# Hybrid encoder step: index products ordered by operand, a new order of the first loads, and two planner constants

## The chip, the cores and the metric

One Trainium2 chip, one core of it. The metric is the device time of one execution of the kernel in microseconds (us). The kernel before was timed three times; the median is the time to compare with.

## What is computed

One layer of a streaming encoder in fp32: 512 prompt tokens and 32 sample tokens of width 1024, 256 memory tokens, and caches of keys and values of the past. One combined input projection feeds three groups of heads and an indexer; the heads' outputs are gated, projected out and added to x.

```python
def _mixer_inputs(x, g, w_in, pos):
    z = _rmsnorm(x, g) @ w_in
    qa, ka, va, ga, qb, kb, vb, gb, qm, gm, qi, ki, wi = _split_cols(z)
...
def _indexer_scores(qi, ki, wi):
    dots = jnp.einsum('bqhd,bsd->bqhs', qi, ki).astype(jnp.float32) * (D_IDX ** -0.5)
    w = wi.astype(jnp.float32) * (H_IDX ** -0.5)
    return jnp.einsum('bqh,bqhs->bqs', w, jax.nn.relu(dots))

def _gather_attend(q, k, v, scores, topk):
    top_val, top_idx = lax.top_k(scores, topk)
...
def _merge(x, oa, ob, om, ga, gb, gm, w_out):
    o = jnp.concatenate([oa * jax.nn.silu(ga), ob * jax.nn.silu(gb), om * jax.nn.silu(gm)], axis=-1)
    return x + o @ w_out
```

Group A is attention over a band of chunks with a position bias, B attends to the keys that the indexer picks, M attends to the memory tokens. Prompt and sample each have all three.

## The kernel before

**Products.** A product of fp32 precision is made of three matmuls. x is split into xTh (rounded, by ScalarE) and xTl (the rest, by VectorE), a weight tile `raw` into wh (ScalarE) and wl (VectorE for the first four pairs of tiles, GpSimd after that); h·wh, h·wl and l·wh are summed in one PSUM bank. The names stand in the rows: `bank<-wl,xTh` is the product of xTh with wl. x and weights have eight tiles of 128 rows along the width of 1024 (index k).

**Order of the work.** The program opens with the index projection (296 columns of `w_in`), which needs all of x: `x_load` sends the eight tiles of x_t (544 columns: 512 prompt, 32 sample) and the eight weight tiles on SP's queue, `x_split` and `w_split` split them, and `index_group` multiplies, for each k, three query tiles of 128 tokens. (The key part of the fourth tile is made apart by `key0` with the scaled weights `gw`.) After it come the input projections of the other groups (the first is ka), each with a small part for the sample tokens by `w_sample` (`bank<-raw,xF`, plain fp32 from the unsplit weights), then attention, and the output projections: the prompt's `bank<-wh,oAh`, `wh,oMh`, `wh,oBh` and the sample's `bank<-raw,oS` (`out_sample`). The sample's group B (`sample_b`) multiplies cached keys, `bank<-keysB,qbS`, that three loads of 512 KB bring in.

**Who sets the order.** The kernel is written out by a planner, `Line`. It keeps an estimated clock for each engine and runs many generators; one emits its next instructions when the planner's clocks say that its inputs are there. The order on each engine's queue is thus fixed when the program is built, by estimates: a DMA is put down with its bytes over 330e3 bytes per us (`Line.op`, line 249), and a PSUM bank counts as free 0.7 us after the estimated end of its last reader (`room` and `there`, lines 462 and 472). On the chip, semaphores keep the order right whatever the estimates were.

**Fillers.** `warm` (line 909) puts matmuls of a tile of ones on TensorE where the planner sees it wait during the index projection, until the time at which the next product is due, and `LATER` = 0.3 us beyond it.

All engine instructions go through one helper, so each row has the line L400; they are told apart by tiles.

Of the kernel before, what the change touches and what calls it, by code (L numbers as in the profile page):

```python
# [18 lines left out]
P = 128  # L19
# [6 lines left out]
NK = 8  # L26
NT = S // P
# [64 lines left out]
class Line:  # L92
# [139 lines left out]
    def op(self, eng, op, outs, ins, kw):  # L232
        deps = {}
        outs_, ins_ = ([x for x in xs if x.tensor.name in self.writes] for xs in (outs, ins))
        for x in outs_ + ins_:
            b = self.box(x)
            for w, o in self.writes[x.tensor.name]:
                if all(p[0] < q[1] and q[0] < p[1] for p, q in zip(w, b)):
                    if o.eng is None:
                        for u in o.users.values():  # L240
                            deps.setdefault(u, False)
                    else:
                        deps[o] = True
        for x in outs_:
            b = self.box(x)
            for (w, _), o in self.reads[x.tensor.name].items():
                if all(p[0] < q[1] and q[0] < p[1] for p, q in zip(w, b)):
                    deps.setdefault(o, False)
        d = (outs[0].size() * 4 / 330e3 if eng == "SP" else
             self.cost(eng, op, outs, ins, kw) * (1.0 if eng == "PE" else SLACK))  # L250
        share = eng == "POOL" or eng == "DVE" and self.shares(op, outs, ins)
        new = Op(eng, d, share, [(o, w) for o, w in deps.items()])
        for x in outs_:
            n, b = x.tensor.name, self.box(x)
            self.writes[n] = [e for e in self.writes[n]
                              if not all(q[0] <= p[0] and p[1] <= q[1] for p, q in zip(e[0], b))] + [(b, new)]
            self.reads[n] = {k: o for k, o in self.reads[n].items()
                             if not all(q[0] <= p[0] and p[1] <= q[1] for p, q in zip(k[0], b))}
        for x in ins_:
            self.reads[x.tensor.name][self.box(x), eng] = new  # L260
        for x in outs_ + ins_:
            self.users[x.tensor.name][eng] = new

        now = self.now()
        for q in self.queue.values():
            while q and q[0].start <= now:
                q.popleft().enter(self.base)
        self.queue[eng].append(new)
        if share and self.queue["POOL" if eng == "DVE" else "DVE"]:
            self.last = self.base.copy()  # L270
            self.events()
        else:
            self.begin(new, self.start(new))
# [155 lines left out]
def hybrid_step(ctx: ExitStack, tc: tile.TileContext, a: dict):  # L429
# [28 lines left out]
    def room(k=1):  # L458

        yield from line.wait(lambda: len(free_banks) >= k)  # L460
        while True:
            t = sorted(pp.free(f"b{b}") for b in free_banks)[k - 1] + 0.7
            if t <= line.now():
                return
            yield t
            yield from line.wait(lambda: len(free_banks) >= k)
# [2 lines left out]
    waiting = []  # L469

    def there(k):
        return k == 0 or len(free_banks) >= k and sorted(pp.free(f"b{b}") for b in free_banks)[k - 1] + 0.7 <= line.now()

    def divided(k, issue):

# [324 lines left out]
    def x_load():  # L800

        c = len(x_raw)
        yield from ()
        t = (rp.tile([P, 2, N], F32, tag="xr", name="xr", bufs=3) if c < 3 else
             cp.tile([P, 2, N], F32, tag="gate1", name="xr"))
        if c % 2 == 0:
            firsts.append(cp.tile([P, 2, 2, 296], F32, tag=("q0", "gate0")[c // 2], name="raw"))
        raw = firsts[c // 2][:, c % 2]
        for kk in range(2):
            rows = slice((2 * c + kk) * P, (2 * c + kk + 1) * P)  # L810
            if c == kk == 0:
                DMA.dma_start(gT[0], a["norm_mix_g"])
            DMA.dma_start(t[:, kk, :], a["x_t"][rows, :])
            DMA.dma_start(raw[:, kk, :], w_in[rows, QI:QI + 296])
        raws.append(raw)
        x_raw.append(t)

# [88 lines left out]
    ones = cp.tile([P, P], F32, tag="q2", name="ones")  # L906
    V.memset(ones, 1.0)

    def warm(until):
        fill, line.warm = line.warm, None  # L910
        until += LATER if until - line.clk["PE"] > WARM else 0
        while until - line.clk["PE"] > WARM:
            PE.matmul(idle[:, 0:P], ones, ones, start=True, stop=True)
        line.warm = fill
# [144 lines left out]
    def index_group():  # L1059
        acc = take(NT)  # L1060
        for c in range(NK // 2):
            w = w_next()
            for kk in range(2):
                k = 2 * c + kk
                line.until(lambda: x_k[0] > k and w_k[0] > k)
                wh, wl = (x[:, kk, :] for x in w)
                for t in range(1, NT):
                    h, l = (x[k // 4][:, k % 4, t * P:(t + 1) * P] for x in (xTh, xTl))
                    o = acc[t][:, 0:296]
                    yield wh, wl, h, l  # L1070
                    PE.matmul(o, h, wh, start=k == 0, stop=False)
                    PE.matmul(o, h, wl, start=False, stop=False)
                    PE.matmul(o, l, wh, start=False, stop=k == NK - 1)
                    if k == NK - 1:
                        line.spawn(i_done(t, acc[t]))
        line.spawn(key0(acc[0]))

    line.spawn(start())
# [1041 lines left out]
```

## Time and profile before

| | us |
|---|---|
| median of 3 runs (353.04, 354.0, 354.1) | 354.0 |
| the profiled execution | 353.58 |
| its span, first to last instruction | 351.8 |
| TensorE (PE) busy | 343.6 (98%) |
| VectorE (DVE) busy | 277.8 (79%) |
| ScalarE (ACT) busy | 220.8 (63%) |
| GpSimd (POOL) busy | 178.7 (51%) |
| mean granted TensorE clock | 0.998 of full speed |

The profile is of one execution; 1.8 us of its time lie outside the span. A row of the timeline gives the start of a group of like instructions, the time from its first start to its last end, the engine and the tiles; matmuls overlap in their pipeline, so the distance of two starts says more than the length of one. In a wait, the arrow names the instruction or DMA that ended it.

### The profile page before, as it was taken

To read this page: it belongs to the slowest core of one execution; us is meant where nothing else is said; L and a number is where in the kernel's file an instruction comes from. 1 tells how busy PE (TensorE), PEld (TensorE's weight loads), DVE (VectorE), ACT (ScalarE), POOL (GpSimd) and SP (SyncE) were. 2 spreads that over 40 slices of the span, in tenths; PEclk is the share of its full clock that TensorE was granted. 3 is DMA by queue.
4 is the path that set the end of the run, shared out by engine and by line. 5 is a ranking of instruction groups with operands and counts; after the bars stand their busy time and mean duration, and the time that the engine had idled before them with its cause. 6 is when DMAs were issued, how large, how long until landed. Compare 5 with 4: busy or idle time off the path is not lost.

```text
span 351.8 us, 7548 instructions
## 1 busy us (share of the span) xinstructions
PE 343.6 (98%) x2744; PEld 299.2 (85%) x2744; DVE 277.8 (79%) x706; ACT 220.8 (63%) x528; POOL 178.7 (51%) x195
## 2 busy tenths in 40 slices
PE   8999999999999999999999999999999999999992
PEld 7989978999999988887988998999986767676782
DVE  3765988878999979998999727999995689786543
ACT  5756777997767776786764328414793377663452
POOL 2569094475575557274654484552382064307542
PEclk9999999999999999999999999999999999999999
DMA  7999452375548223252131341234273185200024
GB/s 241 310 365 352 100 182 60 112 199 149 149 133 286 62 62 113 55 156 85 48 91 45 92 144 42 56 88 144 65 287 133 45 271 176 111 2 2 0 75 178
DMA packets 39604, 46.31 MB, mean 132 GB/s; under 512 B 5360, under 2 KB 32624, under 8 KB 39568
## 3 DMA queue, kind: packets, MB, share of 16 engines
q1 hardware_dynamic: 39568, 45.85, 41.8%
q8 instruction: 21, 0.34, 0.4%
q14 instruction: 15, 0.12, 0.1%
HBM read 39.67 MB, written 6.16 MB: 130 GB/s over the span
## 4 chain that ended last, share of the span: by engine, by line
PE 93%; DMA 3%; issue 1%; SPq 1%; DVE 1%; ACT 0%; POOLq 0%; POOL 0%; DVEq 0%; ACTq 0%
PE bank L400 93%; DMA keysB<-in_cache_b_k_dram 2%; DMA xr<-in_x_t_dram 1%; SPq L400 1%; DVE xr L400 0%; ACT sq L400 0%; POOLq L2108 0%; DVE wl L400 0%; POOL xr L400 0%; POOL ss L400 0%; DVEq L400 0%; ACTq L400 0%
## 5 line engine op out<-in xcount | busy, mean ns | idle before, releaser
L400 POOL TENSOR_TENSOR wl<-raw,wh 128x512 fp32r<-128x512 f32 (+1 forms) x69 | 105.6, 1539 | 80.0 <-ACT wh L400 77.5
L400 ACT ACTIVATE wh<-raw 128x512 fp32r<-128x512 f32 (+2 forms) x77 | 50.4, 660 | 31.1 <-PE bank L400 17.1
L400 PE MATMUL bank<-wh,xTh 128*128 128x384 f32 (+1 forms) x184 | 63.8, 347 | 0.0
L400 PE MATMUL bank<-wl,xTh 128*128 128x384 f32 (+1 forms) x184 | 61.6, 335 | 0.6 <-DVE wl L400 0.6
L400 PE MATMUL bank<-wh,xTl 128*128 128x384 f32 (+1 forms) x184 | 61.0, 332 | 0.0
L400 ACT ACTIVATE z<-z,st 128x384 f32<-128x384 f32 (+3 forms) x80 | 42.4, 549 | 23.9 <-DVE st L400 23.8
L400 PE MATMUL bank<-xTh,wh 128*128 128x272 f32 x208 | 46.1, 303 | 0.0
L400 PE MATMUL bank<-xTh,wl 128*128 128x272 f32 x208 | 43.0, 288 | 0.0
L400 PE MATMUL bank<-xTl,wh 128*128 128x272 f32 x208 | 42.9, 288 | 0.0
L400 PEld LDWEIGHTS bank<-wh,xTh 128*128 128x128 f32 x184 | 34.7, 189 | 2.7 <-issue 2.0
L400 PEld LDWEIGHTS bank<-wl,xTh 128*128 128x128 f32 x184 | 34.6, 188 | 1.2 <-DVE wl L400 0.8
L400 PEld LDWEIGHTS bank<-wh,xTl 128*128 128x128 f32 x184 | 34.7, 188 | 0.0
L400 PEld LDWEIGHTS bank<-xTh,wh 128*128 128x128 f32 x208 | 32.7, 189 | 2.0 <-issue 1.4
L400 PEld LDWEIGHTS bank<-xTl,wh 128*128 128x128 f32 x208 | 32.6, 188 | 0.0
L400 PEld LDWEIGHTS bank<-xTh,wl 128*128 128x128 f32 x208 | 32.5, 189 | 0.0
L400 DVE MAX8 m<-ysel 128x8 f32<-128x256 f32 (+2 forms) x48 | 26.4, 550 | 0.1
L400 DVE MATCH_REPLACE8 ysel<-m,ysel 128x256 f32<-128x256 f32 (+2 forms) x48 | 26.0, 543 | 0.0
L400 PE MATMUL bank<-ident,z 128*128 128x128 f32 (+1 forms) x162 | 25.1, 274 | 0.0
L400 PEld LDWEIGHTS bank<-ident,z 128*128 128x128 f32 (+1 forms) x162 | 18.5, 140 | 5.4 <-issue 2.5
L400 ACT ACTIVATE junkS<-ysS,bi 128x1056 int8<-128x1056 f32 x16 | 18.7, 1170 | 4.3 <-DVE bi L400 4.3
L400 ACT COPY z<-bank 128x384 f32<-128x384 f32 (+2 forms) x26 | 13.2, 511 | 9.5 <-PE bank L400 8.4
L400 POOL TENSOR_TENSOR oBl<-o,oBh 128x128 fp32r<-128x128 f32 (+1 forms) x9 | 5.2, 577 | 27.1 <-ACT oBh L400 27.1
(300 smaller groups left out, 802.5 us busy)
## 6 DMA issues: line engine op xcount, KB each, us to landing
raw<-in_w_in_dram SPq DMA_DIRECT2D x20, 384.0 KB, 3.4
raw<-in_w_in_dram SPq DMA_DIRECT2D x26, 256.0 KB, 2.9
raw<-in_w_out_dram SPq DMA_DIRECT2D x16, 256.0 KB, 4.1
xr<-in_x_t_dram SPq DMA_DIRECT2D x8, 272.0 KB, 4.4
nat<-in_x_prompt_dram SPq DMA_DIRECT2D x4, 512.0 KB, 8.2
raw<-in_w_mem_kv_dram SPq DMA_DIRECT2D x8, 256.0 KB, 3.0
xr<-in_x_prompt_dram SPq DMA_DIRECT2D x4, 512.0 KB, 3.3
out_dram<-xr SPq DMA_DIRECT2D x4, 512.0 KB, 2.6
```

The costliest lines, as they stand in the source:

```text
L400: return fn(*args, **kw)
```

## The change

Five edits. (1) The planner's price of a DMA is its bytes over 200e3 bytes per us while the estimated clock of SP is below 2.5 us, and over 370e3 after that. (2) A bank counts as free 0.4 us after its last reader, not 0.7. (3) The first loads go out as x0, g, raw0, raw1, x1, raw2, x2 and so on, instead of g, x0, raw0, x1, raw1. (4) The first run of fillers ends 0.8 us sooner, and the 0.3 us beyond are added only before 7.5 us of the planner's clock. (5) The index products go by operand: for each k, wh·xTh of the three query tiles, then wl·xTh of the three, then wh·xTl of the three.

```diff
-        d = (outs[0].size() * 4 / 330e3 if eng == "SP" else
+        d = (outs[0].size() * 4 / (200e3 if self.clk["SP"] < 2.5 else 370e3) if eng == "SP" else
...
-            t = sorted(pp.free(f"b{b}") for b in free_banks)[k - 1] + 0.7
+            t = sorted(pp.free(f"b{b}") for b in free_banks)[k - 1] + 0.4
...
-        return k == 0 or len(free_banks) >= k and sorted(pp.free(f"b{b}") for b in free_banks)[k - 1] + 0.7 <= line.now()
+        return k == 0 or len(free_banks) >= k and sorted(pp.free(f"b{b}") for b in free_banks)[k - 1] + 0.4 <= line.now()
...
             if c == kk == 0:
+                DMA.dma_start(t[:, kk, :], a["x_t"][rows, :])
                 DMA.dma_start(gT[0], a["norm_mix_g"])
-            DMA.dma_start(t[:, kk, :], a["x_t"][rows, :])
             DMA.dma_start(raw[:, kk, :], w_in[rows, QI:QI + 296])
+            if c + kk > 0:
+                DMA.dma_start(t[:, kk, :], a["x_t"][rows, :])
...
+    warm_by = [0.8]
+
     def warm(until):
         fill, line.warm = line.warm, None
-        until += LATER if until - line.clk["PE"] > WARM else 0
+        if warm_by and until - line.clk["PE"] > 1.0:
+            until -= warm_by.pop()
+        until += LATER if WARM < until - line.clk["PE"] and until < 7.5 else 0
         while until - line.clk["PE"] > WARM:
             PE.matmul(idle[:, 0:P], ones, ones, start=True, stop=True)
...
-                for t in range(1, NT):
-                    h, l = (x[k // 4][:, k % 4, t * P:(t + 1) * P] for x in (xTh, xTl))
-                    o = acc[t][:, 0:296]
-                    yield wh, wl, h, l
-                    PE.matmul(o, h, wh, start=k == 0, stop=False)
-                    PE.matmul(o, h, wl, start=False, stop=False)
-                    PE.matmul(o, l, wh, start=False, stop=k == NK - 1)
-                    if k == NK - 1:
-                        line.spawn(i_done(t, acc[t]))
+                h, l = (x[k // 4][:, k % 4, :] for x in (xTh, xTl))
+                for x, y in ((h, wh), (h, wl), (l, wh)):
+                    yield x, y
+                    for t in range(1, NT):
+                        PE.matmul(acc[t][:, 0:296], x[:, t * P:(t + 1) * P], y, start=k == 0 and x is h and y is wh,
+                                  stop=k == NK - 1 and x is l)
+                        if k == NK - 1 and x is l:
+                            line.spawn(i_done(t, acc[t]))
```

Since the planner works out the rest of the order from these numbers, the program differs far beyond the lines of the diff. Three places follow.

TensorE (PE) at the start of the program, before; xTh_81 and xTl_83 are the split x, ones the fillers:

```order
L400 MATMUL bank<-ones 128x128 x10
L400 MATMUL bank<-wh,xTh_81 128x296
L400 MATMUL bank<-ones 128x128
L400 MATMUL bank<-wl,xTh_81 128x296
L400 MATMUL bank<-wh,xTl_83 128x296
```

and in the change:

```order
L400 MATMUL bank<-ones 128x128 x9
L400 MATMUL bank<-wh,xTh_81 128x296 x3
L400 MATMUL bank<-wl,xTh_81 128x296 x3
L400 MATMUL bank<-wh,xTl_83 128x296 x3
L400 MATMUL bank<-ones 128x128 x3
L400 MATMUL bank<-wh,xTh_81 128x296 x3
```

One filler fewer stands ahead of the first product, and the nine products of one k stand by operand; over the whole index projection there are 13 fillers where there were 15. Behind the index products the eight `raw,xF 32x296` now stand ahead of the eight `xr,gw`; the eight `raw,xF 32x384` follow, and then ka's products, in both kernels.

TensorE ahead of the sample's group B, before; the load of the keys is released by the last `xTh,wl` above these rows, the last reader of a buffer that SP's load ahead of the keys needs:

```order
L400 MATMUL bank<-ident,z 128x128 x3
L400 MATMUL bank<-wh,oMh 128x512
L400 MATMUL bank<-wh,oMl 128x512
L400 MATMUL bank<-wl,oMh 128x512
L400 MATMUL bank<-keysB,qbS 32x512 x2
```

and in the change:

```order
L400 MATMUL bank<-ident,z 128x128 x3
L400 MATMUL bank<-keysB,qbS 32x512 x2
L400 MATMUL bank<-keysB_3667,qbS 32x512 x2
L400 MATMUL bank<-keysB,qbS 32x512 x2
L400 MATMUL bank<-keysB_3667,qbS 32x512 x2
L400 MATMUL bank<-keysB,qbS 32x32 x2
L400 MATMUL bank<-keysB_3667,qbS 32x32 x2
L400 MATMUL bank<-z,mv 64x128 x16
L400 MATMUL bank<-ident,z 128x128 x3
L400 MATMUL bank<-wh,oMh 128x512
```

The group of three with oMh, a part of the prompt's output projection, has moved from ahead of the keys' products to behind them. The rows between the release and these ones read alike in both kernels.

TensorE between the two `raw,oS 32x512 x4` of the sample's output projection; the four loads for the second are released by the first. Before, the last rows of the stretch:

```order
L400 MATMUL bank<-wh,oAh 128x512
L400 MATMUL bank<-wh,oAl 128x512
L400 MATMUL bank<-wl,oAh 128x512
L400 MATMUL bank<-wh,oMh 128x512
L400 MATMUL bank<-wh,oMl 128x512
L400 MATMUL bank<-wl,oMh 128x512
L400 MATMUL bank<-raw,oS 32x512 x4
```

and in the change:

```order
L400 MATMUL bank<-wh,oAh 128x512
L400 MATMUL bank<-wh,oAl 128x512
L400 MATMUL bank<-wl,oAh 128x512
L400 MATMUL bank<-raw,oS 32x512 x4
```

Before, six such groups of three stand between the two (four with oAh, two with oMh); in the change, five (four with oAh, one with oMh).

## Rows read from the trace of the kernel before

**Rows 1.** The page: span, busy time of each engine, shares of the last-ending chain.

```profile
span 351.8 us, 7548 instructions
PE 343.6 (98%) x2744; PEld 299.2 (85%) x2744; DVE 277.8 (79%) x706; ACT 220.8 (63%) x528; POOL 178.7 (51%) x195
...
PE 93%; DMA 3%; issue 1%; SPq 1%; DVE 1%; ACT 0%; POOLq 0%; POOL 0%; DVEq 0%; ACTq 0%
```

**Rows 2.** Busy time by stretch; behind the columns' names, one row for each stretch.

```profile
core 0: us, PE busy (x) PEld busy (x) DVE busy (x) ACT busy (x) POOL busy (x), PEclk, DMA share, GB/s
0.00:5.30 5.30, 4.25 (x20) 4.25 (x21) 0.62 (x2) 2.57 (x4) 1.79 (x13) 1.00 0.54 150
5.30:17.70 12.40, 11.81 (x84) 11.32 (x83) 9.47 (x18) 9.29 (x16) 5.72 (x9) 1.00 1.01 329
17.70:20.85 3.15, 3.15 (x51) 1.50 (x49) 2.87 (x6) 0.35 (x2) 2.65 (x2) 1.00 1.03 386
20.85:258.00 237.15, 237.06 (x1892) 218.72 (x1891) 201.52 (x520) 157.49 (x373) 129.57 (x126) 1.00 0.42 126
...
342.80:351.80 9.00, 2.78 (x24) 2.58 (x23) 3.51 (x8) 2.34 (x6) 1.98 (x3) 0.93 0.43 175
```

**Rows 3.** What TensorE waited for, whole program: us in total, times, longest.

```profile
PE bank L400 <- DVE ones L400: 1.1, 1, 1.1
PE bank L400 <- DVE wl L400: 0.6, 1, 0.6
PE bank L400 <- DMA keysB<-in_cache_b_k_dram: 0.2, 1, 0.2
```

**Rows 4.** Timeline of TensorE, index projection: start, us, instructions, idle before and releaser.

```profile
1.05 4.63 PE L400 MATMUL bank<-ones 128*128 128x128 f32 x20 [1.05 <-DVE ones L400]
5.33 0.59 PE L400 MATMUL bank<-wh,xTh 128*128 128x296 f32 x1
...
7.27 0.40 PE L400 MATMUL bank<-wh,xTh 128*128 128x296 f32 x1
8.26 0.41 PE L400 MATMUL bank<-wl,xTh 128*128 128x296 f32 x1 [0.59 <-DVE wl L400]
...
9.61 0.61 PE L400 MATMUL bank<-ones 128*128 128x128 f32 x4
9.97 0.39 PE L400 MATMUL bank<-wl,xTh 128*128 128x296 f32 x1
...
17.78 0.64 PE L400 MATMUL bank<-xr,gw 128*32 128x128 f32 x16
18.24 2.68 PE L400 MATMUL bank<-raw,xF 128*32 128x296 f32 x32
20.85 0.44 PE L400 MATMUL bank<-wh,xTh 128*128 128x384 f32 x1
```

**Rows 5.** Timeline of SP's queue: the first loads, and the last two weights for ka.

```profile
0.73 0.38 SPq L400 DMA_DIRECT2D g_mix<-in_norm_mix_g_dram  x1
1.17 0.42 SPq L400 DMA_DIRECT2D xr<-in_x_t_dram  x1
...
13.39 0.88 SPq L400 DMA_DIRECT2D raw<-in_w_in_dram  x2
```

**Rows 6.** DMA issued at 13.80 (second of that pair): KB, us to landing.

```profile
raw<-in_w_in_dram SPq DMA_DIRECT2D x1, 384.0 KB, 6.2
```

**Rows 7.** Timeline of TensorE around the sample's group B.

```profile
262.90 0.48 PE L400 MATMUL bank<-wh,oMh 128*128 128x512 f32 x1
...
263.77 1.05 PE L400 MATMUL bank<-keysB,qbS 64*32 64x512 f32 x4
265.06 1.91 PE L400 MATMUL bank<-keysB,qbS 64*32 64x512 f32 x16 [0.25 <-DMA keysB<-in_cache_b_k_dram]
```

**Rows 8.** The chain that ended last, in order of time, at the same place: start, us.

```profile
258.85 0.43 SPq L400
...
259.32 5.70 DMA keysB<-in_cache_b_k_dram
```

**Rows 9.** Timeline of TensorE, sample's output projection.

```profile
277.85 1.06 PE L400 MATMUL bank<-raw,oS 128*32 128x512 f32 x8
278.85 0.66 PE L400 MATMUL bank<-ident,qb 128*128 128x128 f32 x4
...
280.47 0.39 PE L400 MATMUL bank<-wh,oMh 128*128 128x512 f32 x1
...
281.16 0.40 PE L400 MATMUL bank<-wh,oAh 128*128 128x512 f32 x1
...
284.07 1.76 PE L400 MATMUL bank<-raw,oS 128*32 128x512 f32 x8
285.75 0.33 PE L400 MATMUL bank<-k,q 64*128 64x128 f32 x2
```

**Rows 10.** The loads for its second part: SP's queue, and the last one's us to landing.

```profile
278.96 1.75 SPq L400 DMA_DIRECT2D raw<-in_w_out_dram  x4
...
raw<-in_w_out_dram SPq DMA_DIRECT2D x1, 256.0 KB, 4.4
```

## The prediction

> **What bounds the kernel.** I read the page first. TensorE is busy for 343.6 of 351.8 us and holds 93% of the chain that ended last; the rest of the chain is 3% DMA and crumbs [rows 1]. So the kernel can only become faster where TensorE stands still, and slower where it is made to. The table by stretches says where that is [rows 2]: from 20.85 to 258 us it is idle for 0.09 of 237 us. What it stands still for lies in the first 18 us, at two places late in the program, and in the last 9 us, whose order the change leaves alone. The waits of TensorE name only three [rows 3]: the tile of ones at the very start, one wl, one load of keys. A fourth has no wait of its own in that view, and the timeline shows it, the second `raw,oS` (below).
>
> **The index projection.** It runs from 5.33 to 17.78 us [rows 4], 12.45 us. Its 72 products start about 0.137 us apart where nothing is in the way (from 8.51 to 9.61 there are eight of them in 1.10 us), so 9.9 us of it are products. The other 2.6 us are one pause (products at 7.27 and 8.26 with nothing between: 0.99 less a product, 0.85 us, ended by wl of the second k), fillers inside it (0.36 us for two at 9.61), and switches between fillers and products.
>
> The change does three things here. The ten first fillers hold TensorE from 1.05 to 5.33, 0.43 us each; nine end at about 4.9, but the first product also needs xTh and wh of tile 0, whose weights are issued at 1.63 as before. I take a start at 5.15, so 0.2 us. Second, raw1 goes out ahead of x1 and wl of the second k stands behind three wh products, so the pause of 0.85 goes. Third, two of the later fillers' places go, some 0.3 us at 0.18 us a filler. Sum: the projection ends about **1.3 us** sooner, near 16.4.
>
> What comes behind it decides whether that counts. The small products `raw,xF` with 384 columns need the four weight tiles of ka, and ka's own products follow them at 20.85 [rows 4]. The last of the four tiles is issued at 13.80 and lands 6.2 us later, at 20.0 [rows 5, 6]. ka starts 0.82 us after that landing, with only the last of the small products between; TensorE was already on the heels of its loads. In that stretch and the one before it the DMA engines are busy all the time (share 1.01 and 1.03) at 329 and 386 GB/s [rows 2], so the landing can't move by an order of TensorE. It moves only by how much sooner the stream begins: x0 is issued at 0.73 instead of 1.17, as g gives it the first place [rows 5]. That is at most 0.44 us, and at least nothing, since g then takes its turn and all later issues keep theirs. I take 0.3, in the middle and with a crumb for the last products, which stand in line when the tile lands. So of 1.3 us gained **0.3** stay, with bounds of 0 and 1.3, and TensorE pauses for about 1 us near 19.
>
> **The keys of the sample's group B.** The three loads are issued at 258.85 and after, behind a load released by the last xTh product. The second is issued at 259.32 and lands 5.70 us later, at 265.02, and TensorE goes on at 265.06 [rows 7, 8]. That landing hangs on a release which stands the same number of instructions earlier in both kernels. Ahead of it the group of three with oMh, 262.90 to 263.77, filled 0.87 us of the waiting [rows 7]. The change puts that group behind the keys. So TensorE comes 0.87 us sooner, waits as much longer, and makes the group after it: **+0.7**. That is 0.87 less the little that the keys' first products need before the tile that is late; the bounds are 0.69, what such a group takes where it stands among others (280.47 to 281.16 [rows 9]), and 0.87.
>
> **The second part of the sample's output projection.** The four loads for it are issued from 278.96 on, when the first part is made; the last takes 4.4 us and lands at about 284.7 [rows 10]. The first part of eight matmul records takes 1.00 us to the next start, 277.85 to 278.85; the second takes 1.68, 284.07 to 285.75 [rows 9]. The 0.68 us between them is waiting for the last tile, which the view of waits does not show since the records before it stand in the pipeline. The change leaves five groups between the two parts where six were. One takes 0.69 us (280.47 to 281.16) [rows 9], and the loads hang on the first part. So the wait grows by **0.7**; the bounds are 0 (if loads land sooner, with less other traffic) and 0.7.
>
> **The bank margin and the DMA price.** Both only change the planner's estimates. A smaller margin puts a bank's next user up to 0.3 us nearer to its last reader. In the trace TensorE never waits for an evicting engine after the start [rows 3], and from 20.85 to 258 us all its pauses add to 0.09 us [rows 2], so there is slack at nearly all places; I take 0, with 0 and +0.6 as bounds (two pauses of 0.3). The two sample outputs and some loads of weights and biases change places on SP's queue; in the same long stretch the DMA engines are busy for 0.42 of the time [rows 2], and that covers them.
>
> **One rule against the change.** TensorE's granted clock is 1.00 in each stretch up to 342.8 us and falls only in the last, to 0.93, where TensorE is idle for 6.2 of 9.0 us [rows 2]. The pause of 0.85 us at the second k left it at 1.00. The change makes three pauses of about 1 to 1.5 us, longer than that one. The Trainium skill, "TensorE: Matmul & The Clock Gate", section "HAM oscillation — how this bites in real kernels", holds that idle gaps of TensorE, if long enough, take the clock back to its lower level, and that the work after them then runs slow. By that rule fewer fillers and a new pause would be a risk, with the sum of the third rival below; the trace agrees for the last stretch alone and shows nothing of it at the pauses before.
>
> **The sum.** Against the profiled execution, 353.58 us: −0.3 + 0.7 + 0.7 = +1.1, so 354.7. That execution lies 0.4 below the median of the runs, 354.0, from which the same sum gives 355.1; I put the time between the two, **354.9**. A measurement of this kernel tells a difference of about 0.3%, 1.06 us, from none, so this is at the edge of what can be seen.
>
> **Rivals.**
>
> *The early gain carries through.* If the ka tiles land early enough, or TensorE gets 1.3 us out of it otherwise, the sum is −1.3 + 1.4 = +0.1: about 354.0. For it: the loads of ka wait in SP's queue for earlier ones, and a faster index stage could release them. Against it: the busy DMA engines [rows 2]. 18%.
>
> *The late waits do not grow.* Loads land sooner, or the planner's moves elsewhere fill them: −0.3 to −1.3 alone, 352.3 to 353.3 from the profiled execution, so 352.5 to 353.5, halfway to the median as above. For it: the landing of the keys took 5.70 us for 512 KB, a long time that depends on other traffic [rows 8]. Against: SP's order there is the same. 20%.
>
> *The clock falls in a new pause.* The price is bounded by the start, where the first fillers take 0.43 us each against 0.18 (0.36 for two) later [rows 4]: if as long a stretch as that one, 4.3 us, ran at that ratio behind the pause at 19, it would cost up to 2.4 us: 356 to 357.3. It decides once the pause is long enough for the chip to lower the clock, and no pause of before up to 1 us was. 7%.
>
> *Banks come too late.* The margin was what kept TensorE from waiting for ScalarE and VectorE; two or three places with 0.3 us each add to my forecast, 355.5 to 355.9. For it: ScalarE and VectorE are busy for 157 and 202 of the 237 us [rows 2], so an eviction can be late. Against: no such wait shows. 8%.
>
> **How the numbers follow.** My forecast has 47%, with its own range of 354.0 to 355.7 (early gain 0 to 0.44, late waits 0.7 to 1.6). Faster than 352.9 is most of the second rival (14%), a little of the first (4%) and of the forecast (2%): 20%. Slower than 355.1 is the upper part of the forecast (21%) and the last two rivals (15%): 36%. The rest, 44%, is no difference that can be told. The range from 352.7 to 356.2 leaves out the lower end of the second rival, the clock, and the ends of others, about 2 in 10.
>
> **What the profile of the change will show.** The first product near 5.1 us and the last index product near 16.4; no wait for wl of the second k; a pause of TensorE near 19 us that ends with the last weight tile of ka, and ka's products starting at about 20.5. The wait for the keys grows to about 1 us by the view of waits or the timeline, with the oMh group behind it. The second `raw,oS` takes about 2.4 us to the next start instead of 1.68. TensorE's busy sum stays within 1 us of 343.6, its clock 1.00. I am wrong if ka starts at 19.6 or sooner (the loads did not bind), if the second `raw,oS` or the keys wait no longer than before, or if TensorE waits for an eviction between 21 and 258 us.

## The result and the profile after

The change makes the kernel slower: 356.68 us in the median of 7 runs (355.56 to 358.52) against 354.28 of 7 runs of the kernel before on the same chips (353.04 to 355.35). The ratio is 1.0067, with a 95% interval of 1.0040 to 1.0094. The forecast was 354.9, with a range that ended at 356.2. The profiled execution took 356.04 us against 353.58, so 2.46 us are to be found.

What TensorE waits for in the change (us in total, times, longest); before there were three, for ones, for wl and for the keys [rows 3]:

```profile
PE bank L400 <- DMA keysB<-in_cache_b_k_dram: 1.2, 1, 1.2
PE bank L400 <- DVE ones L400: 1.1, 1, 1.1
PE bank L400 <- ACT wh L400: 0.4, 1, 0.4
PE bank L400 <- DMA raw<-in_w_in_dram: 0.4, 2, 0.2
PE bank L400 <- DVE st L400: 0.3, 1, 0.3
PE bank L400 <- ACT ka L400: 0.3, 1, 0.3
```

The wait for wl of the second k is gone, as the change meant it to be. A wait for wh has come ahead of the first product, one for ka's weight tiles behind the index projection, the wait for the keys is almost five times as long (1.16 us for 0.25), and two waits for ScalarE and VectorE, `ka` and `st`, are new: those two end the reading of PSUM banks that TensorE wants next.

The timeline of TensorE in the change shows where these waits lie. Its first part answers to [rows 4]:

```profile
1.05 4.21 PE L400 MATMUL bank<-ones 128*128 128x128 f32 x18 [1.05 <-DVE ones L400]
5.67 1.10 PE L400 MATMUL bank<-wh,xTh 128*128 128x296 f32 x3 [0.41 <-ACT wh L400]
...
16.50 0.56 PE L400 MATMUL bank<-wh,xTl 128*128 128x296 f32 x3
16.99 1.20 PE L400 MATMUL bank<-raw,xF 128*32 128x296 f32 x16
18.01 0.62 PE L400 MATMUL bank<-xr,gw 128*32 128x128 f32 x16
18.45 0.83 PE L400 MATMUL bank<-raw,xF 128*32 128x384 f32 x8
19.49 0.84 PE L400 MATMUL bank<-raw,xF 128*32 128x384 f32 x4 [0.21 <-DMA raw<-in_w_in_dram]
20.48 0.84 PE L400 MATMUL bank<-raw,xF 128*32 128x384 f32 x4 [0.15 <-DMA raw<-in_w_in_dram]
21.25 0.45 PE L400 MATMUL bank<-wh,xTh 128*128 128x384 f32 x1
...
40.03 0.34 PE L400 MATMUL bank<-wl,xTh 128*128 128x384 f32 x1
40.64 0.84 PE L400 MATMUL bank<-identR,stk 32*128 32x32 f32 x8 [0.28 <-ACT ka L400]
...
146.22 0.28 PE L400 MATMUL bank<-xTh,wh 128*128 128x272 f32 x1
146.84 0.39 PE L400 MATMUL bank<-xTh,wh 128*128 128x272 f32 x1 [0.34 <-DVE st L400]
```

The index products end 0.8 us sooner (behind 16.99, before 17.78), although they begin 0.34 us later, since the first product waits for wh of the first weight tile. All of that and more is lost by 21.25, where ka's products start, 0.40 us after the 20.85 of before. The two pauses at 40 and 146 us, 0.28 and 0.34 us of idle, stand between starts that lie 0.61 and 0.62 us apart.

The second part answers to [rows 7, 9]; it is the same view:

```profile
259.03 0.42 PE L400 MATMUL bank<-xTh,wl 128*128 128x272 f32 x2
...
264.23 1.05 PE L400 MATMUL bank<-keysB,qbS 64*32 64x512 f32 x4
266.44 1.97 PE L400 MATMUL bank<-keysB,qbS 64*32 64x512 f32 x20 [1.16 <-DMA keysB<-in_cache_b_k_dram]
268.34 1.97 PE L400 MATMUL bank<-z,mv 128*64 128x128 f32 x32
...
281.94 2.10 PE L400 MATMUL bank<-raw,oS 128*32 128x512 f32 x8
283.96 0.33 PE L400 MATMUL bank<-k,q 64*128 64x128 f32 x2
```

And the kernel before at two of these places, for comparison: its last product that reads xTh ahead of the keys, and the first one behind the keys' products:

```profile
258.02 0.42 PE L400 MATMUL bank<-xTh,wl 128*128 128x272 f32 x2
...
266.96 0.55 PE L400 MATMUL bank<-z,mv 128*64 128x128 f32 x6
```

So the 2.46 us come as follows. By the start of ka +0.40. From there to the last product that reads xTh, 237.17 us before and 237.78 now: +0.61; both kernels have 1892 matmul records there, and the idle of the two pauses at 40 and 146 us is 0.62. The keys' block, from its first product to `z,mv`, 3.19 us before (263.77 to 266.96) and 4.11 now (264.23 to 268.34): +0.92. The second `raw,oS`, 1.68 before and 2.02 now (281.94 to 283.96): +0.34. That is 2.27. Between these places six groups of three of the prompt's output projection have moved: the stretches that they left are 4.06 us shorter and the one from 283.96 to the end is 4.19 longer, +0.13. The last 0.06 lie outside the span.

### The profile page after: what moved, and what is told of

Same layout as the page of the kernel before. It is cut to its first block, busy times and chain, and to the rows that moved or that the text cites. A ratio compares the mean times of both kernels' runs of the same rounds, so it can differ in the third digit from the quotient of the medians.

```text
span 354.2 us, 7576 instructions
## 1 busy us (share of the span) xinstructions
PE 344.4 (97%) x2740; PEld 299.3 (84%) x2740; DVE 278.4 (79%) x699; ACT 223.5 (63%) x533; POOL 177.1 (50%) x198
## 4 chain that ended last, share of the span: by engine, by line
PE 84%; DVE 5%; DMA 5%; ACT 1%; issue 1%; POOL 1%; SPq 0%; POOLq 0%; DVEq 0%; ACTq 0%
PE bank L400 84%; DMA raw<-in_w_in_dram 3%; DMA keysB<-in_cache_b_k_dram 2%; DVE rt L400 1%; DVE z L400 1%; DVE ysel L400 1%; DVE m L400 1%; ACT wh L400 1%; POOL wl L400 1%; DVE rot L400 1%; SPq L400 0%; DVE xr L400 0%; DVE bi L400 0%; DVE rotS L400 0%; DVE queried L400 0%
## 5 line engine op out<-in xcount | busy, mean ns | idle before, releaser
L400 POOL TENSOR_TENSOR wl<-raw,wh 128x512 fp32r<-128x512 f32 (+1 forms) x69 | 102.5, 1494 | 70.8 <-ACT wh L400 66.6
L400 PE MATMUL bank<-wh,xTh 128*128 128x384 f32 (+1 forms) x184 | 61.5, 349 | 0.4 <-ACT wh L400 0.4
L400 PE MATMUL bank<-wl,xTh 128*128 128x384 f32 (+1 forms) x184 | 58.6, 332 | 0.0
L400 PE MATMUL bank<-wh,xTl 128*128 128x384 f32 (+1 forms) x184 | 58.5, 332 | 0.0
L400 ACT ACTIVATE z<-z,st 128x256 f32<-128x256 f32 (+3 forms) x80 | 42.3, 551 | 23.8 <-DVE st L400 23.7
L400 PEld LDWEIGHTS bank<-wh,xTl 128*128 128x128 f32 x184 | 33.8, 189 | 0.1
L400 DVE SCALAR_TENSOR_TENSOR ysel<-r,wI,ysel 128x256 f32<-128x256 f32 (+2 forms) x21 | 19.0, 904 | 4.1 <-ACT r L400 3.4
L400 ACT COPY z<-bank 128x384 f32<-128x384 f32 (+2 forms) x31 | 15.8, 512 | 8.3 <-PE bank L400 7.6
```

The costliest lines, as they stand in the source:

```text
L400: return fn(*args, **kw)
```

## Experiments

The planner makes another program of every small edit, so an edit alone does not isolate its effect. Seven of the fourteen kernels below therefore keep the planner's order of one kernel, instruction for instruction, and only issue a few of them in another order: the planner is told the old order, and the instructions are held and sent out in the new one (`hold` and `flush` in the diffs). Each run was timed against runs of the kernel before on the same chip; the ratio is to these, with its 95% interval in brackets.

### The early stage alone, in three parts

Loads in the new order, on the order of before (e_loads):

```diff
+        DMA.hold = []
         for kk in range(2):
...
             DMA.dma_start(raw[:, kk, :], w_in[rows, QI:QI + 296])
+        DMA.flush((1, 0, 2, 4, 3) if c == 0 else (1, 0, 3, 2))
```

> The kernel before with its whole order kept, but the first loads issued as x0, g, raw0, raw1, x1, raw2, x2 and so on. Theory L (the order of the first loads makes the stream of loads later, and ka's products wait for it): the last weight tile of ka lands near 20.4 us instead of 20.0, ka's products start at 21.1 to 21.3 us, and the run is 0.3 to 0.5 us slower than before. Rival I (the later start of ka comes of the products by operand and the fewer fillers): ka starts at 20.85 as before or up to 0.4 us sooner, and the run is within 0.1 us of before or faster.

Measured: ratio 1.0001 (0.9980 to 1.0023). In its profile the last weight tile of ka landed at 21.2 us, later than anywhere else, and ka started at 21.95. The time is what rival I expected; that start of ka neither did.

The products by operand (for seven of the eight k) and two fillers fewer, on the order and the loads of before (e_index):

```diff
+                    PE.hold = later if k < NK - 1 else None
                     PE.matmul(o, h, wh, start=k == 0, stop=False)
                     PE.matmul(o, h, wl, start=False, stop=False)
                     PE.matmul(o, l, wh, start=False, stop=k == NK - 1)
...
+                if k < NK - 1:
+                    PE.hold = later
+                    PE.flush((0, 3, 6, 1, 4, 7, 2, 5, 8))
```

> The kernel before with its whole order kept, loads included, but for seven of the eight k the nine index products by operand, and two fillers fewer (the tenth, and the one between the first products). Theory L: the pause at the second k grows shorter and the index projection ends 0.5 to 1.3 us sooner, but ka's last tile lands at 20.0 as before and ka starts at 20.7 to 20.85; the run is 0 to 0.15 us faster. Rival I: ka starts near 21.2 and the run is 0.3 to 0.5 us slower. A third way, in which the loads of ka move with the index projection, would give ka at 20.2 or sooner and 0.6 us or more.

Measured: ratio 0.9989 (0.9974 to 1.0005). ka started at 21.70, later than any of the three theories had it, though the loads were issued in the order of before.

Both together (e_early):

> Both edits of the two runs above together, all else in the order of before: the early stage of the change with the late order of before. Theory L: ka starts near 21.2, the run is 0.3 to 0.5 us slower than before, and the waits for the keys (0.25 us) and for the second small output product are as before. Rival E (the late waits grow because the early stage shifts the engines against each other): the run is 2 us slower or more, as the change is.

Measured: ratio 0.9994 (0.9979 to 1.0010); ka at 21.53. This is not in all respects the early stage of the change. ScalarE keeps the order of before, in which it splits x1 ahead of the second weight tile, while the change has it split that weight tile first; x1 now lands later, and TensorE waits for wh:

```profile
7.93 0.67 PE L391 MATMUL bank<-wh,xTh 128*128 128x296 f32 x3 [1.14 <-ACT wh L410]
```

The index products ended at 18.08 in this profile (before 17.78, the change 16.99), so it has no early gain that could be waited away.

Against 20.85 in before all three starts of ka look late, and yet the times are those of before. With the old order of loads ka started at 20.85 (before), 21.70 (e_index), 21.20 (e_late, below) and 20.81 (b_keys, below), with the new one at 21.25, 21.95 and 21.53: the landing of the last tile varies by a microsecond between executions of like loads. Theory L's cost of 0.3 to 0.5 us for the new order of loads is thus neither shown nor ruled out by the traces, and the times of e_early leave it between 0.74 us faster and 0.35 us slower than before. By these runs it is worth nothing that can be told, and the loss must come later.

### The late order alone (e_late)

The change with its own late order, the first loads and the index products issued as before; its 13 fillers and ScalarE's order stay those of the change (the diff shows the index products alone):

```diff
+                    PE.hold = later
                     for t in range(1, NT):
                         PE.matmul(acc[t][:, 0:296], x[:, t * P:(t + 1) * P], y, start=k == 0 and x is h and y is wh,
...
+                PE.hold = later
+                PE.flush((0, 3, 6, 1, 4, 7, 2, 5, 8))
```

> The change with its whole late order kept, but the first loads issued in the order of before and the index products issued tile by tile. The theory that most of the loss is in the order that the planner made of the new constants: ka starts at 20.85 to 21.0, the wait for the keys is 1.1 us or more, the pauses near 40 and 146 us stay, and the run is 1.7 to 2.2 us slower than before. Rival E: the run is within 0.5 us of before and the late waits are those of before.

Measured: ratio 1.0063 (1.0041 to 1.0085), the 1.0067 of the change within the intervals. As far as these can tell, the loss is all in the order that the planner made behind the index projection. In this profile the index products ended at 17.60 us and ka started at 21.20; in the change they ended at 16.99 and ka started at 21.25: the 0.6 us by which the change is ahead there are gone by the start of ka. Rival E falls from both sides, by this run and by e_early. The profile of this run also shows one pause at its dearest; TensorE at 40 us:

```profile
40.12 0.34 PE L410 MATMUL bank<-wl,xTh 128*128 128x384 f32 x1
41.81 0.82 PE L410 MATMUL bank<-identR,stk 32*128 32x32 f32 x8 [1.35 <-ACT ka L410]
...
42.93 0.52 PE L410 MATMUL bank<-wh,xTl 128*128 128x384 f32 x1
43.25 0.52 PE L410 MATMUL bank<-wl,xTh 128*128 128x384 f32 x1
```

and its busy time by stretch, the granted clock behind POOL's busy time:

```profile
40.00:42.00 2.00, 0.65 (x6) 0.33 (x4) 1.90 (x8) 2.00 (x6) 0.00 (x0) 1.00 0.60 172
42.00:44.00 2.00, 2.00 (x13) 1.97 (x13) 1.62 (x5) 2.00 (x5) 0.27 (x1) 0.68 0.00 0
44.00:46.00 2.00, 2.00 (x10) 1.90 (x9) 0.25 (x1) 2.00 (x7) 2.00 (x2) 0.50 0.23 84
46.00:48.00 2.00, 2.00 (x20) 1.55 (x23) 0.63 (x3) 2.00 (x4) 1.39 (x3) 0.97 0.87 313
```

The pause that took 0.28 us of idle in the change takes 1.35 here, and behind it the products stand 0.32 us apart where they stood 0.175 apart: the granted clock is 0.50, which is 1.2 GHz, from 44 to 46 us. The clock's share, an estimate from these rows, is 2 us times 0.32, 0.50 and 0.03, some 1.7 us. This happened in the profiled execution, whose mean granted clock was 0.991; the other five of e_late had 0.994 to 0.997. The profile of the change has 1.00 behind its pause:

```profile
41.00:44.00 3.00, 3.00 (x23) 2.90 (x22) 1.49 (x4) 3.00 (x7) 1.43 (x2) 1.00 0.00 0
```

### The keys' loads ahead of the loads of x (a_keys, b_keys)

On the change and on the kernel before, orders kept, only these six loads change places on SP's queue; the second and third load of keys still wait for the last product that reads xTh, but no load of x of 512 KB goes ahead of them:

```diff
+    DMA.hold = []
     for t in range(NT - 1):
         DMA.dma_start(xr[t], a["x_prompt"][t * P:(t + 1) * P, :])
...
         for m, t in enumerate(kt):
             DMA.dma_start(t[:, 0:PAST], a["cache_b_k"][m * P:(m + 1) * P, :])
...
+        DMA.flush((3, 4, 5, 0, 1, 2))
```

> The change with its whole order kept, but the three loads of the sample's group B keys are issued ahead of the three loads of x that stood in front of them. Theory K (the keys' landing sets that place, and the group of three that left it is paid in waiting): the second load of keys lands at 263.5 to 264.5 us of the span instead of 266.4, the wait for the keys falls from 1.2 to under 0.3 us, and the run is 0.8 to 1.3 us faster than the change (1.0 to 1.5 us slower than before). Rival D (what is gained there is lost at the next load): the wait for the keys goes but the second small output product waits as much longer, and the run is as slow as the change.

Measured on the change: ratio 0.9964 (0.9943 to 0.9985), so 1.0% under the change and under the kernel before too. The second load of keys was issued at 259.59 us and landed 3.5 us later, at 263.1, where it took 6.06 us in the change. The wait for the keys is gone from the view of waits, and the block runs through:

```profile
264.19 1.98 PE L410 MATMUL bank<-keysB,qbS 64*32 64x512 f32 x24
266.10 1.09 PE L410 MATMUL bank<-z,mv 128*64 128x128 f32 x16
```

1.91 us from its first product to `z,mv` where the change takes 4.11: the wait cost 2.2 us, though its longest idle stretch is 1.16. While the keys of one tile are missing, the products of the others go two at a time instead of four, and that is slow work that counts as busy. The first records of the block show it, in the change and then in a_keys; in both kernels the next start comes 0.43 to 0.45 us behind them:

```profile
264.23 0.62 PE L400 MATMUL bank<-keysB,qbS 64*32 64x512 f32 x2
...
264.19 0.63 PE L410 MATMUL bank<-keysB,qbS 64*32 64x512 f32 x4
```

> The kernel before with the same edit, the loads of the keys ahead of the three loads of x. Theory K: the wait of TensorE for the keys, about 0.8 us between starts, goes, and the run is 0.5 to 0.8 us faster than before. Rival D: no gain, within 0.2 us of before.

Measured on the kernel before: ratio 0.9936 (0.9911 to 0.9961). There the block falls from 3.19 to 1.91 us. What theory K says of the wait holds on both kernels, and rival D falls. Its sizes were too small: it expected 0.8 to 1.3 us and 0.5 to 0.8 us, the block in the traces gives 2.2 and 1.3 us, and the times give about 3.6 us (2.4 to 4.9) and 2.3 us (1.4 to 3.2). So the times gained somewhat more than one trace of each explains; what the rest comes of stays open.

### The two planner constants (a_marg, b_marg, b_price)

The bank margin of 0.7 us in the change, of 0.4 in the kernel before, and the new price of a DMA alone in the kernel before (the diff is that of a_marg, one of two like places):

```diff
-            t = sorted(pp.free(f"b{b}") for b in free_banks)[k - 1] + 0.4
+            t = sorted(pp.free(f"b{b}") for b in free_banks)[k - 1] + 0.7
```

> The change with the bank margin back at 0.7 us, the other edits kept; the planner makes another order of it. Theory B (the smaller margin puts users of a bank so near its last reader that TensorE waits for late evictions): no pause of TensorE for ScalarE or VectorE over 0.15 us between 25 and 255 us, and from the start of ka's products to the last product that reads xTh the pauses add up to less than 0.1 us as before. Rival P (such pauses come of the DMA price or of luck in the order): one or more pauses of 0.2 us or more for ScalarE or VectorE stay. The time can go either way by the loads further on, 353.5 to 357 us.

Measured: ratio 0.9911 (0.9890 to 0.9931), 352.09 us, the fastest kernel here and under the range that both theories gave. Against the change it is 1.55% faster, some 5.5 us (4.3 to 6.7). No wait for an eviction is left:

```profile
PE bank L400 <- DVE ones L400: 1.1, 1, 1.1
PE bank L400 <- DMA raw<-in_w_in_dram: 0.9, 2, 0.7
PE bank L400 <- POOL wl L400: 0.5, 1, 0.5
PE bank L400 <- ACT wh L400: 0.3, 1, 0.3
```

The keys and the second `raw,oS` wait for nothing in this order either (1.00 us for the latter, the length of the first part). From the profile of the change to this one the keys' block is 2.2 us shorter, the second `raw,oS` 1.0, the two pauses are gone (0.6), and ka starts 0.45 later.

> The kernel before with the bank margin of 0.4 us alone; the planner makes another order of it. Theory B: pauses of TensorE for ScalarE or VectorE of 0.2 us or more between 25 and 255 us, as in the change (0.28 and 0.34 us there), of which before has none. Rival P: none. The time can go either way by the loads further on, 353.5 to 357 us.

Measured: ratio 1.0118 (1.0098 to 1.0138), 359.48 us, over the range that both theories gave. Waits for evictions are there, and late weights for `raw,oS` with them:

```profile
PE bank L400 <- ACT z L400: 1.6, 2, 1.2
PE bank L400 <- DMA raw<-in_w_out_dram: 1.4, 2, 1.0
...
PE bank L400 <- DVE z L400: 0.6, 1, 0.6
```

By these two alone theory B would stand. The missing corner says otherwise:

> The kernel before with the new price of a DMA alone, bank margin 0.7 as before; the planner makes another order of it. Theory B (the margin is what brings the waits for evictions): no pause of TensorE for ScalarE or VectorE over 0.2 us between 25 and 255 us, and a time of 352 to 356 us, by the waits for loads alone. Rival D2 (the price, under which the planner thinks that loads land sooner, brings pauses or late loads by itself): pauses of 0.3 us or more in that stretch, or a time of 356 us or more.

Measured: ratio 1.0116 (1.0084 to 1.0148), with the margin at 0.7:

```profile
PE bank L400 <- ACT z L400: 1.4, 3, 0.6
...
PE bank L400 <- DVE gate L400: 0.8, 1, 0.8
PE bank L400 <- ACT ka L400: 0.6, 1, 0.6
```

Three of its waits for ScalarE and VectorE, of 0.4 to 0.6 us, lie between 25 and 255 us, and the one for `ka`, at 41 us, stands ahead of the same `identR,stk` products as the pause of the change at 40 us. So the price brings such waits as well as the margin. Neither constant is good or bad by itself: each alone costs the kernel before 1.2%. And b_price, at 1.0116, differs from a_marg, at 0.9911, in the three early edits alone. On a kept order these gave nothing that can be told; handed to the planner, they make another order behind them, here one that is 2.0% faster.

### Other margins on the change (a_m55, a_m85)

> The change with the bank margin at 0.55 us. Theory B (too small a margin makes TensorE wait for evictions, by the sum of the pauses): between the margins of 0.4 (2.4 us over before) and 0.7 (3.1 us under before): fewer or shorter pauses for ScalarE and VectorE between 25 and 255 us than in the change, and none or one over 0.2 us. Rival P (each constant gives another order, and which loads it happens to be late for sets the time): pauses for evictions and waits for loads that follow no line with the margin; the time may be anywhere from 351 to 359.

Measured at 0.55 us: ratio 1.0313 (1.0292 to 1.0334), far slower than at 0.4 and, at 365.83 us, over the range of both theories. Its rows by stretch around the dearest pause (1.97 us of idle, ended by `DVE st`, up to 180.68):

```profile
178.00:180.00 2.00, 0.71 (x6) 0.50 (x4) 1.90 (x8) 1.42 (x4) 0.53 (x1) 1.00 0.21 78
180.00:184.00 4.00, 3.32 (x12) 3.32 (x13) 3.92 (x16) 2.59 (x10) 1.29 (x1) 0.67 0.34 96
```

> The change with the bank margin at 0.85 us. Theory B: no pause for ScalarE or VectorE over 0.2 us between 25 and 255 us, as at 0.7. Rival P: such pauses come back. The time is set by the loads that this order happens to be late for, 351 to 357 us by both.

Measured at 0.85 us: ratio 0.9951 (0.9936 to 0.9966), with pauses of 0.5 us for `ACT z` and 0.3 for `ACT bf_ok`, against theory B. By margin, 0.4, 0.55, 0.7 and 0.85, the change stands at 1.0067, 1.0313, 0.9911 and 0.9951: the time follows no line with the margin, and rival P, that each constant gives another order whose waits follow none of the constants, fits best. What is left of theory B is a tendency at most: the three orders made with a margin under 0.7 are all slower than before and all wait for evictions, but so does b_price, at 0.7.

### The tables behind ka's weight tiles (e_tables, am_all, am_keys)

To test that ka's weight tiles wait away the early gain, the tables that go out ahead of them are sent behind them. On e_early:

```diff
+            if what != "w" and late:
+                DMA.hold, late = late, None
+                DMA.flush(range(5))
...
+                DMA.hold = late = []
                 load_tables(32)
                 DMA.dma_start(gT[1], a["norm_mem_g"])
+                DMA.hold = None
```

> The early stage of the change on the late order of before, as in an earlier run, and one edit more: the four tables and a gain that SP sends ahead of ka's four weight tiles go behind them. Theory L2 (the early gain is real but is waited away at ka's weight tiles, whose landing the stream of loads sets): the last of the four tiles lands at 17 to 18.5 us instead of 20 to 21, the pause of TensorE behind the index products goes or falls under 0.3 us, ka's products start at 19.0 to 20.0 us, and the run is 0.8 to 1.8 us faster than before. Rival S (the stream is as long whatever the order, or the tables come too late for what reads them): ka starts at 20.5 or later, or a new wait behind it takes the gain back, and the run is within 0.4 us of before.

Measured: ratio 1.0003 (0.9989 to 1.0016). The last tile landed at 17.9 us and ka started at 20.66, with no wait for the tiles; but 2.4 us later, behind twelve products, TensorE waited 0.66 us for `ACT k`. Where the tile is there, the small products themselves stand between; and the index products ended at 17.80 in this profile, as in before (17.78), so here too no early gain was there to be kept.

> The change with the bank margin at 0.7, with the loads of the keys ahead of the loads of x, and with the tables behind ka's weight tiles: a try for a version that beats both kernels. It was 3.1 us faster than before with the margin alone; its order has hardly a wait for the keys, so that edit should give 0 to 0.2 us here, and the tables 0.8 to 1.8 us by theory L2: 4 to 5 us faster than before, some 350 to 351.5 us. By rival S it is where the margin alone put it, 351.5 to 352.5.

Measured: ratio 0.9979 (0.9968 to 0.9990), slower than the margin alone and, at 353.87 us, over both ranges expected. ka started at 19.23, as theory L2 said, and then:

```profile
21.26 0.34 PE L410 MATMUL bank<-wl,xTh 128*128 128x384 f32 x1
23.97 0.44 PE L410 MATMUL bank<-wh,xTh 128*128 128x384 f32 x1 [2.37 <-ACT k L410]
```

VectorE's row says why:

```profile
18.83 0.46 DVE L410 TENSOR_TENSOR rt<-bank,sin 128x288 f32<-128x288 f32 x1 [3.93 <-DMA sin<-in_sin_dram]
```

The rotation of the index rows waits 3.9 us for the sine table. ScalarE waits for the rotations in its turn, and its copy of `k` out of a bank, which ends TensorE's wait, stands behind that on its queue:

```profile
22.58 0.18 ACT L410 ACTIVATE wI<-bank 128x8 f32<-128x8 f32 x1 [1.24 <-DVE rot L410]
...
23.67 0.25 ACT L410 COPY k<-bank 128x128 f32<-128x128 f32 x1
```

Both halves hold: L2 for the landing, rival S for the time. The same copy is a second limit on the early gain even where the tables go first: in the profile of before it ends at 22.74 us, and the thirteenth product of ka, the one that waits for it in am_all and in e_tables, starts at 23.05. A ka that came over 0.3 us sooner would have waited there, unless the copy came sooner too; in the change, whose index products end 0.8 us sooner, it ends at 22.97, no sooner.

> The change with the bank margin at 0.7 and the loads of the keys ahead of the loads of x, tables where they were. In the order of that margin TensorE hardly waits for the keys (0.46 us from the first to the second of their products, as where they are there), so theory K expects the time of the margin alone within 0.3 us: 0.8 to 1.0% under before. If it is faster by more, the loads' order helps elsewhere too; if it is as slow as 353.5 us, the try with the tables lost by this edit and not by the tables.

Measured: ratio 0.9944 (0.9919 to 0.9969), 352.68 us. Its interval overlaps that of the margin alone, from which the middle is 0.33% away; whether the keys' edit costs something here is not settled, and it gains nothing where nothing waits for keys. From here to am_all the tables lost another 0.35% (0.08 to 0.62).

## Why the prediction was wrong

**The step that failed is the bank margin**, "I take 0". The argument was that before has no wait for an evicting engine and 0.09 us of pauses in 237 us, so there would be slack at nearly all places. That says that the order of before is good; it says nothing of the new order, in which other users stand behind other evictions. The change has two such pauses, the last of the signs by which the prediction said it would be wrong, +0.61 us together, the size that the fourth rival gave to two or three of them (it had 8%). And the margin decides more than these: put back at 0.7 with the other four edits kept (a_marg), the planner's order loses both pauses and the late waits too, and the run is 1.55%, some 5.5 us, faster than the change. The cause was named too narrowly: the runs show the price of a DMA to bring such waits too, and the pause at 40 us stands in b_price with the old margin. What brings the one at 146 us stays open.

**The keys.** The mechanism was right, and a_keys shows it: the products arrive sooner and wait for a landing. The term was 0.7 and measured 0.92, over its upper bound of 0.87, and by two misses that hide each other: counted from the last product that reads xTh, TensorE came only 0.55 us sooner (5.20 instead of 5.75), not 0.87, and the landing came 0.36 us later (7.36 instead of 7.00, with the second load 6.06 us on its way instead of 5.70). What was not seen is that the waiting block also runs its products two by two, so that this place cost the kernel before 1.3 us, not the 0.25 of its row.

**The second `raw,oS`.** Forecast +0.7, measured +0.34. The loads landed sooner: the last of the four took 4.0 us where it was 4.4. But in six profiles with the late order of before the stretch takes 1.00 to 2.19 us (before 1.68, e_loads 1.00, e_index 1.57, e_early 2.19, b_keys 1.50, e_tables 1.10), in three with that of the change 1.87 to 2.02. So a single pair says little about 0.3 us, and this term is neither shown nor refuted.

**The early stage.** That ka's weight tiles would wait the gain away agrees with the profile of the change: products 0.8 us sooner, two waits for `raw` behind them, and ka no sooner; e_late beside it says the same. The forecast of 16.4 for the end of the index products was too early by 0.6 us: the first product came at 5.67 and not at 5.15, since it waited for wh of the first tile, and of the later fillers one went, not two. Whether the −0.3 stayed can't be told: e_early gives −0.2 us, with −0.74 and +0.35 as bounds, and ka, 0.40 later in the profile of the change, moves by more than that between executions. x0 did go out 0.44 us sooner, but ka's last tile landed at 20.4, no sooner than the 20.0 of before.

**The sum.** −0.3 + 0 + 0.7 + 0.7 was forecast; +0.40, +0.61, +0.92, +0.34 came in the one pair of profiles. Each term was off by less than 0.8 us, but three of four to the same side. The first and the last lie within what executions of one order differ by, so of the four the bank term is the miss that the runs bear out.

**The clock.** The third rival, 7%, did not decide the change's profile, which shows a clock of 1.00 at all its pauses. But e_late's pause at the same place as the change's brought the clock to its lower level (1.2 GHz) for 3 to 4 us, so it may take part in other executions of the change than the profiled one; that is not shown, and the mean granted clock of the seven, 0.994 to 0.999, is in none as low as e_late's 0.991. The Trainium skill, "TensorE: Matmul & The Clock Gate", section "HAM oscillation — how this bites in real kernels", says that idle gaps lead to slow work behind them; e_late agrees (clock 0.50 behind 1.35 us of idle) and so does a_m55 (0.67 behind 1.97), the profile of am_all does not (1.00 behind 2.37).

## What to carry to other kernels

Where a planner's estimates set the order, treat a changed constant as a new program: a trace without waits says that its order fits, not that there is slack for another. To learn what an edit does by itself, keep the emitted order and change only the issue of the instructions in question; here that showed of five edits that the three early ones give nothing that can be told on a kept order, and that the loss is in the order that the planner made of all of them. And look at a busy stretch for products that run two at a time for want of one operand: in the kernel before the wait for the keys was worth five times its idle row (1.28 us for 0.25), and moving three loads ahead of three others was worth 0.6% on the kernel before.

## What the hardware showed that was not expected

The landing of the same loads in the same order moved by about 1 us between executions of kernels that share it: ka's last tile was issued at 13.8, 13.9 and 14.3 us in the profiles of before, b_keys and e_index, and landed at 20.0, 20.0 and 20.9; with the order of the change, in its own profile and those of a_marg and a_m85, it was issued at 13.9, 14.0 and 14.0 and landed at 20.4, 20.9 and 21.0. And the granted clock did not follow the length of the pause alone: 1.35 us of idle with nothing but plain products ahead and behind brought it to 0.50 (e_late), 2.37 us left it at 1.00 in the profile of am_all, where all rows from 23 to 30 us show 1.00:

```profile
23.00:25.00 2.00, 1.03 (x6) 1.03 (x7) 0.46 (x1) 1.97 (x5) 1.44 (x1) 1.00 1.02 259
25.00:27.00 2.00, 2.00 (x13) 2.00 (x12) 0.76 (x3) 2.00 (x4) 1.46 (x3) 1.00 1.09 347
```

Other executions of am_all may differ in this: five of its twelve have a mean granted clock of 0.990 to 0.992, where the kernel before on the same chip has none under 0.994. Only the profiled one, at 0.998, has a trace.
